# Hymba layer on one core: two partial-sum copies swap tiles every other step, gate sigmoids one slot earlier in the second half

## The chip, the cores and the metric

One Trainium2 chip, one of its cores. The metric is the device time of one execution in microseconds (us); a kernel's time is the median of its runs. The engines are TensorE (PE for its matmuls, PEld for its weight loads), VectorE (DVE), ScalarE (ACT), GpSimd (POOL) and SyncE (SP, which here issues almost all DMAs). Every engine works through its own instructions in the order in which the program lists them; an instruction that waits holds back all that stand behind it on its engine.

## What is computed

A decoder layer with two groups of token mixers (sequence 2048, width 1024, float32). The shapes: x is 2048 x 1024, w_in 1024 x 6144, w_out 2048 x 1024.

```python
xn = rms_norm(x, ln_g)
b_gate, c_gate, x_conv, g_conv, x_lru, g_lru = split(xn @ w_in)      # six of 1024 columns
y_conv = b_gate * causal_conv3(c_gate * x_conv)
u = causal_conv4(x_lru) + lru_conv_b
r = sigmoid(block_diag(u, w_a) + b_a); i = sigmoid(block_diag(u, w_i) + b_i)   # 16 heads of 64
a = exp(8 * r * log_sigmoid(lam))
h_t = a_t * h_{t-1} + sqrt(1 - a_t^2) * (i_t * u_t)                  # scan over the sequence
y = concat(head_norm(y_conv) * silu(g_conv), head_norm(h) * silu(g_lru))
out = rms_norm(x + y @ w_out, final_g)
```

## The kernel before

**Steps.** The work is a list of steps, numbered n. The first 48 are the input projection: 24 for the first half of the sequence and 24 for the second. They come in triples `l`, `a`, `b`, eight triples to a half (k = 0 to 7): `l` makes 128 channels of x_lru and g_lru, `a` of c_gate and x_conv, `b` of b_gate and g_conv. Sixteen steps of kind `o` follow, the output projection. Everything is channels by time, so a step's result is two blocks of 128 channels by 1024 positions. Its four quarters are named 11, 12 (the first block, first and second 512 positions), 21 and 22 (the second block).

**A step is a 2 x 2 block product by Winograd's form of Strassen's scheme:** seven products numbered 0 to 6 rather than eight, on sums and differences of blocks. The left blocks (weights, tiles `s`, a ring of 7) and the right blocks (activations, tiles `th` and `tl`) are each split into a high and a low part, so that a product is 4 x 3 = 12 matmuls of 128x128 by 128x512 (line 924, `mm`). One product takes one *slot* of the loop. In an ordinary step the slots s = 0 to 6 do product 0, product 6 *of the step before*, then 1, 3, 2, 4, 5. The first three of a step go into PSUM bank `A` one upon the other, and the partial sums of the scheme are copied out of it by ACT on the way:

- after product 0 into `q1` (line 1229),
- after product 1 into `u2` (line 1232; the page calls this tile `u`, and so also another tile of that name, the recurrence's),
- after product 2 into `rr` (line 1235).

DVE reads these copies when it puts the quarters together (`put`): quarter 22 is bank `B` plus `rr`, in slot 4; 11 is `C` plus `q1`, in slot 5; 21 is `B` plus `u2` when product 6 is in, which is in slot 1 *of the next step*. Each of the three copies has one tile (`sm(tag)`: a pool with one buffer per name). So the copy into `u2` in slot 2 of a step may start only when DVE has made quarter 21 of the step before, and as bank `A` is added to further, product 2 on PE (slot 4) starts only after that copy has read it. DVE's quarter 21 appears in the profile as `gl<-bank,u`, `xx<-bank,u`, `gb<-bank,u` or `ob<-bank,u` (after an `l`, `a`, `b` or `o` step).

A few steps at a change of the right blocks run otherwise: one with eight plain block products and no partial sums (`opens`), and the one behind it, with six slots (`late`).

**Order of everything else.** The scheduler is told to keep the order in which the code is written. `tick()` at the start of each slot runs what has fallen due: `at(n, f)` runs f at the n-th tick from now, and things due at one tick run in the order in which they were registered. Then come the preparations of the next step's left blocks (`prep`: in the first half ACT casts and DVE or POOL subtractions, with the split tiles stored to `sd`; in the second half mostly loads of `sd`), then the slot's matmuls, then the copy or `put`.

**The gates.** When `put(12)` of an `l` step is done (its slot 6), `lru` books its whole recurrence by such ticks (lines 753 to 759): the convolution at 1 to 3, `sth` and `stl` (the split of u into tiles `st`, ACT and DVE) at 5 and 6, `gates(0)` at 8, `sigs(0)` at 9, `gates(1)` at 10, `sigs(1)` at 11, then tanh, exp, sqrt and the scan. Tick 8 is slot 0 of the `b` step, tick 11 its slot 3. `gates(i)` is four matmuls into two PSUM tiles (line 704, pool `pss`, two buffers); `sigs(i)` is four sigmoids on ACT, r, i, r, i (line 711), the first two reading the first of these tiles and the last two the second. `gates(1)` takes the same two PSUM buffers, so it waits for `sigs(0)`.

A SiLU gate is a sigmoid on ACT (`sg`, line 637), two ticks after quarter 21, and a multiplication on POOL (`gb<-gb,sg`, `gl<-gl,sg`).

Of the kernel before, what the change touches and what calls it, by code (L numbers as in the profile page):

```python
# [38 lines left out]
def hymba_kernel(ctx: ExitStack, tc: tile.TileContext, x, xt, w_in, par, lamc, w_gate, w_out, final_g, out):  # L39
# [282 lines left out]
    def hl_done(n):  # L322
        hlc[0] -= n
# [338 lines left out]
    def lru(h, k, late=0):  # L662
        o1 = wt("o1", "xl", n=N2 + 4)
        g = wt("o2", "gl", bufs=O2)
        if h == 0:
            nc.gpsimd.memset(o1[:, 0:4], 0.0)
        else:
            nc.scalar.copy(o1[:, 0:4], hx[:, k, :])
        v = {}
        lw = [pt[:, LW + 8 * j + k:LW + 8 * j + k + 1] for j in range(4)]  # L670

        def c0():
            v["u"] = wt("u", "u")
            nc.scalar.activation(out=v["u"], in_=o1[:, 1:1 + N2], func=AF.Identity, scale=lw[0],  # L674
                                 bias=pt[:, LB + k:LB + k + 1])

        def cj(j):
            nc.vector.scalar_tensor_tensor(out=v["u"], in0=o1[:, 1 + j:1 + j + N2], scalar=lw[j],  # L678
                                           in1=v["u"], op0=ALU.mult, op1=ALU.add)

        def keep():
            if h == 0:
                nc.scalar.copy(hx[:, k, :], o1[:, N2:N2 + 4])

        def sth():
            v["st"] = st = hl_tile("st", 2)
            at(6, lambda: hl_done(2))
            for j, hi in enumerate((LO, HI)):
                nc.scalar.copy(st[j][hi], v["u"][hi])

        def stl():
            st = v["st"]
            for j, (hi, lo) in enumerate(((LO, HI), (HI, LO))):
                tt(st[j][lo], v["u"][hi], st[j][hi].bitcast(F32), ALU.subtract)

        def gates(i):
            sl = slice(i * C, (i + 1) * C)
            if i == 0:
                v["r"], v["i"] = wt("r", "r"), wt("ig", "i", bufs=IG)
            v["ps"] = ps = []  # L700
            for j in range(2):
                ps.append(pss.tile([P, C], F32, tag="s", name="gate"))
                for n in range(2):
                    nc.tensor.matmul(ps[j], v["gw"][n][:, j, :], v["st"][j][:, sl],  # L704
                                     start=(n == 0), stop=(n == 1))

        def sigs(i):
            sl = slice(i * C, (i + 1) * C)
            for j, (hi, lo) in enumerate(((LO, HI), (HI, LO))):
                for g_, src, bias in ((v["r"], hi, BA), (v["i"], lo, BI)):  # L710
                    nc.scalar.activation(out=g_[hi, sl], in_=v["ps"][j][src], func=AF.Sigmoid,  # L711
                                         bias=pt[src, bias + k:bias + k + 1])


        def s0():
            tt(v["u"], v["i"], v["u"], ALU.mult)

        def s1():
            v["T"] = wt("ig", "T", bufs=IG)
            nc.scalar.activation(out=v["T"], in_=v["r"], func=AF.Tanh, scale=nklam[:, k:k + 1])  # L720

        def s1b():
            nc.scalar.activation(out=v["r"], in_=v["r"], func=AF.Exp, scale=klam[:, k:k + 1])

        def s2():
            nc.scalar.activation(out=v["T"], in_=v["T"], func=AF.Sqrt)

        def s3():
            nc.vector.scalar_tensor_tensor(out=v["u"], in0=v["r"], scalar=1.0, in1=v["u"],
                                           op0=ALU.add, op1=ALU.mult)  # L730

        def s4():
            tt(v["u"], v["T"], v["u"], ALU.mult)

        def s5():
            r = v["r"]
            init = 0.0 if h == 0 else hl[:, k:k + 1]
            nc.vector.tensor_tensor_scan(out=r, data0=r, data1=v["u"], initial=init,
                                         op0=ALU.mult, op1=ALU.add)
            if h == 0:  # L740
                nc.vector.tensor_copy(hl[:, k:k + 1], r[:, N2 - 1:N2])

        def out_():
            finish(0, h, KT + k, v["r"], g, pt[:, LG + k:LG + k + 1])

        def gw():
            v["gw"] = load_gate_w(k)

        def put(which, bank, other):
            dst = {11: o1[:, 4:4 + C], 12: o1[:, 4 + C:4 + N2], 21: g[:, 0:C], 22: g[:, C:N2]}[which]  # L750
            combine(dst, bank, other)
            if which == 12:
                at(1, c0)
                at(2, lambda: cj(1), lambda: cj(2), keep, gw)
                at(3, lambda: cj(3))
                for slots, *fs in ((5, sth), (6, stl), (8, lambda: gates(0)), (9, lambda: sigs(0)),
                                   (10, lambda: gates(1)), (11, lambda: sigs(1)), (12, s1, s0),
                                   (13, s1b), (14, s2, s3), (15, s4), (16, s5), (17, out_)):
                    at(slots + late, *fs)
            if which == 21:  # L760
                silu(g, late)

        return put
# [71 lines left out]
    sm_u2 = [None]  # L835
# [96 lines left out]
    def sm(tag):  # L932
        return small.tile([P, C], F32, tag=tag, name=tag)
# [29 lines left out]
    with tc.manual_schedule(engines={ENG.PE, ENG.Activation, ENG.DVE, ENG.Pool, ENG.SP}):  # L963
# [182 lines left out]
        for n in range(PLAIN, N):  # L1146
            kind, h, k = steps[n]
# [27 lines left out]
            slots = (0, 6) + ORDER[1:] if not late else AFTER  # L1175
            for s in range(6 if late else 8 if new or last else 7):
                i = slots[s]
                place[0] = {"l": 0, "a": 7, "b": 14}.get(kind, 0) + s
                tick()
                if soon and s == 3:  # L1180
                    T2 = {}
                    change = Change(set_of(n + 2), T2)
                if soon and s > 3:
                    change.slot(s - 8)
                if new:
                    change.slot(s)
                if late:
                    change.slot(16 + s)
                    if s == 0:
                        prep(n, 7)  # L1190
                elif n > 0 and opens(n - 2):
                    if s == 0:
                        prep(n, 5)
                        prep(n, 6)
                    elif s == 2:
                        prep(n, 7)
                elif s == 0:
                    prep(n, 6)
                elif s == 2:
                    prep(n, 7)  # L1200
                if new and s > 0:
                    if s in (1, 3, 4, 5):
                        prep(n + 1, (1, 3, 4, 5).index(s) + 1)
                    elif s > 5:
                        prep(n + 2, s - 5)
                elif s > 0:
                    prep(n + 1, s - 1)
                if s == 3:
                    load_next(n + 2)
                if s == 1 and not late:  # L1210
                    if pend is not None:
                        S6, B, put0, u20 = pend
                        alone = B is None
                        if alone:
                            B = bank()
                        for j in range(NB):
                            mm(B, S6, T, 6, j, alone and j == 0, j == NB - 1, not alone)
                        put0(21, B, u20)
                        pend = None
                    continue  # L1220
                b = {0: "A", 1: "A", 2: "A", 5: "D" if late else "A", 3: "B", 6: "B", 4: "C"}[i]
                first = b not in bk
                if first:
                    bk[b] = bank()
                for j in range(NB):
                    mm(bk[b], S_, T, i, j, first and j == 0, j == NB - 1, not first)
                if i == 0:
                    q1 = sm("q1")
                    nc.scalar.copy(q1, bk["A"])  # L1229
                elif i == 1:  # L1230
                    u2 = sm_u2[0] = sm("u2")
                    nc.scalar.copy(u2, bk["A"])  # L1232
                elif i == 2:
                    rr = sm("rr")
                    nc.scalar.copy(rr, bk["A"])  # L1235
                    put(22, bk["B"], rr)
                    if late:
                        put(12, bk["D"], rr)
                elif i == 4:
                    put(11, bk["C"], q1)  # L1240
                elif i == 5 and not late:
                    put(12, bk["A"], None)
                elif i == 6:
                    put(21, bk["B"], u2)
# [50 lines left out]
```

## Time and profile before

| | |
|---|---|
| median of 3 runs | 1357.18 us (1356.16 to 1359.64) |
| the profiled execution, its own time | 1361.65 us |
| its span, first to last instruction | 1359.8 us |
| mean granted TensorE clock | 0.989 |
| PE busy in the span | 1301.9 us (96%) |
| DVE, ACT, POOL busy | 1032.5, 748.4, 226.2 us |
| bytes moved | 355.28 MB, 77.1% of the 16 DMA engines' time |

The durations below are from the profiled execution. It took 4.5 us longer than the median of the runs, and 1.85 us of its time lie outside the span. In rows of the trace the first number is the start in us, the second the duration; a bracket at the end gives the idle time of that engine before the row and what ended it. A row of the waits gives who waited for whom, the total in us, how many times, and the longest. A row of a table by stretch gives, behind the stretch and its length, the busy us and instruction counts of PE, PEld, DVE, ACT and POOL, the granted clock, the DMA share and GB/s.

### The profile page before, as it was taken

To read this page: it belongs to the slowest core of one execution; us is meant where nothing else is said; L and a number is where in the kernel's file an instruction comes from. 1 tells how busy PE (TensorE), PEld (TensorE's weight loads), DVE (VectorE), ACT (ScalarE), POOL (GpSimd) and SP (SyncE) were. 2 spreads that over 40 slices of the span, in tenths; PEclk is the share of its full clock that TensorE was granted. 3 is DMA by queue.
4 is the path that set the end of the run, shared out by engine and by line. 5 is a ranking of instruction groups with operands and counts; after the bars stand their busy time and mean duration, and the time that the engine had idled before them with its cause. 6 is when DMAs were issued, how large, how long until landed. Compare 5 with 4: busy or idle time off the path is not lost.

```text
span 1359.8 us, 16618 instructions
## 1 busy us (share of the span) xinstructions
PE 1301.9 (96%) x5648; PEld 1058.6 (78%) x5648; DVE 1032.5 (76%) x1245; ACT 748.4 (55%) x1139; POOL 226.2 (17%) x160
## 2 busy tenths in 40 slices
PE   6989999999999999899999999999999799998997
PEld 5867877777878787777888888888878688887886
DVE  7778788789989897978566676667458776759885
ACT  7475757575665757565544645364456233444443
POOL 3204242333334340101010110101000000000000
PEclk9989999999999999999999999999999899999999
DMA  7137797988879888542789999999778889797643
GB/s 284 31 119 258 270 252 273 278 296 302 319 281 330 291 291 304 173 162 79 247 304 286 335 354 331 332 339 365 228 253 313 249 236 227 271 404 260 240 146 136
DMA packets 158805, 355.28 MB, mean 261 GB/s; under 512 B 17920, under 2 KB 52736, under 8 KB 158720
## 3 DMA queue, kind: packets, MB, share of 16 engines
q1 hardware_dynamic: 158432, 353.90, 77.1%
q8 instruction: 45, 0.74, 0.2%
q14 instruction: 40, 0.33, 0.1%
q10 hardware_dynamic: 288, 0.32, 0.1%
HBM read 217.11 MB, written 137.04 MB: 260 GB/s over the span
## 4 chain that ended last, share of the span: by engine, by line
PE 40%; DMA 7%; DVE 4%; ACT 3%; issue 1%; SPq 0%; DVEq 0%; ACTq 0%
PE bank L924 40%; DMA traw<-td 1%; DMA zr<-rsd 1%; PE gate L704 1%; ACT i L711 1%; ACT r L711 1%; DVE tl L163 1%; DMA traw<-in_w_out_dram 1%; DMA od<-xr 1%; DMA xr<-od 1%; DVE s L163 1%; DMA xr<-in_x_dram 1%; ACT th L435 1%; DMA yd<-gl 0%; DMA raw<-yd 0%
## 5 line engine op out<-in xcount | busy, mean ns | idle before, releaser
L924 PE MATMUL bank<-th,s 128*128 128x512 f32 x3632 | 1138.8, 392 | 19.9 <-ACT u L1232 10.0
L924 PEld LDWEIGHTS bank<-th,s 128*128 128x128 f32 x3632 | 686.1, 189 | 173.5 <-ACT u L1232 15.0
L924 PE MATMUL bank<-tl,s 128*128 128x512 f32 x1816 | 711.1, 392 | 1.6 <-DVE tl L163 1.3
L924 PEld LDWEIGHTS bank<-tl,s 128*128 128x128 f32 x1816 | 343.2, 189 | 74.8 <-DVE tl L163 3.5
L163 POOL TENSOR_TENSOR s<-raw,s 128x512 fp32r<-128x512 f32 x62 | 110.2, 1790 | 253.9 <-ACT s L200 210.7
L200 ACT CAST s<-raw 128x512 fp32r<-128x512 f32 x140 | 84.5, 616 | 75.4 <-PE bank L924 41.8
L163 DVE TENSOR_TENSOR tl<-traw,th 128x512 fp32r<-128x512 f32 x117 | 85.1, 763 | 40.4 <-ACT th L435 30.0
L1232 ACT COPY u<-bank 128x512 f32<-128x512 f32 x58 | 34.0, 586 | 145.6 <-PE bank L924 77.8
L163 DVE TENSOR_TENSOR s<-s,s 128x512 fp32r<-128x512 f32 x105 | 95.5, 909 | 10.5 <-ACT s L200 10.5
L163 POOL TENSOR_TENSOR gb<-gb,sg 128x1024 f32<-128x1024 f32 x16 | 40.6, 2537 | 348.3 <-ACT sg L637 328.2
L163 DVE TENSOR_TENSOR s<-raw,s 128x512 fp32r<-128x512 f32 (+1 forms) x125 | 92.7, 765 | 6.5 <-ACT s L982 4.4
L200 ACT CAST s<-s 128x512 fp32r<-128x512 f32 x105 | 64.7, 616 | 30.3 <-DVE s L163 25.8
L435 ACT CAST th<-traw 128x512 fp32r<-128x512 f32 x96 | 55.1, 618 | 30.7 <-DMA traw<-td 17.8
L1229 ACT COPY q<-bank 128x512 f32<-128x512 f32 x58 | 33.9, 584 | 68.0 <-PE bank L924 59.2
L678 DVE SCALAR_TENSOR_TENSOR u<-xl,pt,u 128x1024 f32<-128x1024 f32 x48 | 62.7, 1306 | 6.3 <-ACT u L674 5.7
L163 DVE TENSOR_TENSOR raw<-raw,zr 128x512 f32<-128x512 f32 x64 | 41.2, 684 | 34.6 <-DMA zr<-rsd 31.1
L1235 ACT COPY rr<-bank 128x512 f32<-128x512 f32 x58 | 33.8, 583 | 50.4 <-PE bank L924 50.4
L788 DVE SCALAR_TENSOR_TENSOR t<-p,pt,t 128x1024 f32<-128x1024 f32 x32 | 46.5, 1454 | 5.9 <-ACT t L785 5.1
L163 DVE TENSOR_TENSOR st<-u,st 64x1024 fp32r<-64x1024 f32 x32 | 46.5, 1452 | 1.0
L711 ACT ACTIVATE r<-gate,pt 64x512 f32<-64x512 f32 x64 | 43.8, 684 | 3.1 <-PE gate L704 2.4
L163 POOL TENSOR_TENSOR gl<-gl,sg 128x1024 f32<-128x1024 f32 x16 | 40.4, 2523 | 24.5 <-ACT sg L637 24.5
L711 ACT ACTIVATE i<-gate,pt 64x512 f32<-64x512 f32 x64 | 43.8, 684 | 1.1
(153 smaller groups left out, 1153.7 us busy)
## 6 DMA issues: line engine op xcount, KB each, us to landing
sd<-s SPq DMA_DIRECT2D x151, 512.0 KB
s<-sd SPq DMA_DIRECT2D x151, 512.0 KB
raw<-in_w_in_dram SPq DMA_DIRECT2D x104, 256.0 KB
raw<-yd SPq DMA_DIRECT2D x64, 256.0 KB
traw<-in_w_out_dram SPq DMA_DIRECT2D x64, 256.0 KB
so<-so SPq DMA_DIRECT2D x22, 512.0 KB
s<-so SPq DMA_DIRECT2D x22, 512.0 KB
yd<-gl SPq DMA_DIRECT2D x32, 256.0 KB
```

The costliest lines, as they stand in the source:

```text
L163: (eng or nc.vector).tensor_tensor(out=out, in0=a, in1=b, op=op)
L200: nc.scalar.copy(dst[i][0], val(i))
L435: nc.scalar.copy(self.dst[i, j][0], self.r[i, j])
L678: nc.vector.scalar_tensor_tensor(out=v["u"], in0=o1[:, 1 + j:1 + j + N2], scalar=lw[j], in1=v["u"], op0=ALU.mult, op1=ALU.add)
L704: nc.tensor.matmul(ps[j], v["gw"][n][:, j, :], v["st"][j][:, sl], start=(n == 0), stop=(n == 1))
L711: nc.scalar.activation(out=g_[hi, sl], in_=v["ps"][j][src], func=AF.Sigmoid, bias=pt[src, bias + k:bias + k + 1])
L788: nc.vector.scalar_tensor_tensor(out=tcur["t"], in0=p[:, 2 + j:2 + j + N2], scalar=cw[j], in1=tcur["t"], op0=ALU.mult, op1=ALU.add)
L924: nc.tensor.matmul(bank, a[:, js], b, start=start and n == 0, stop=stop and n == 2, skip_group_check=more)
L1229: nc.scalar.copy(q1, bk["A"])
L1232: nc.scalar.copy(u2, bk["A"])
L1235: nc.scalar.copy(rr, bk["A"])
```

## The change

Two edits. In odd steps the two tiles of the third and fourth copies change places: `u2` is kept in the tile `rr`, and `rr` in the tile `u2`. And with h = 1 (the second half of the sequence) the two calls of `sigs` are booked one tick earlier, at 8 and 10, which are the ticks of `gates(0)` and `gates(1)`; as they are registered behind these, they stand behind them.

```diff
-                for slots, *fs in ((5, sth), (6, stl), (8, lambda: gates(0)), (9, lambda: sigs(0)),
-                                   (10, lambda: gates(1)), (11, lambda: sigs(1)), (12, s1, s0),
+                for slots, *fs in ((5, sth), (6, stl), (8, lambda: gates(0)), (9 - h, lambda: sigs(0)),
+                                   (10, lambda: gates(1)), (11 - h, lambda: sigs(1)), (12, s1, s0),
...
-                    u2 = sm_u2[0] = sm("u2")
+                    u2 = sm_u2[0] = sm(("u2", "rr")[n % 2])
                     nc.scalar.copy(u2, bk["A"])
                 elif i == 2:
-                    rr = sm("rr")
+                    rr = sm(("rr", "u2")[n % 2])
                     nc.scalar.copy(rr, bk["A"])
```

No instruction is added or taken away. On PE, POOL and SP the order is the same row for row. On ACT and DVE the first edit changes names only: this is ACT in step 3, the first step with seven products (`s<-raw`, `s<-s` are casts of left blocks, `xrow` is the norm of later rows, `r<-r` a square for the head norm):

```order
 L200 CAST s<-raw 128x512 x2
-L1232 COPY u_1075<-bank 128x512
+L1232 COPY rr<-bank 128x512
 L200 CAST s<-s_1051 128x512
 L534 ACTIVATE xrow,ss_615<-xrow 128x1024
 L200 CAST s<-raw 128x512
-L1235 COPY rr<-bank 128x512
+L1235 COPY u_1122<-bank 128x512
 L629 ACTIVATE r<-r 128x1024
```

The place in the order stays, the tile is the other one. This is DVE some way behind it, in slot 1 of step 4, where quarter 21 of step 3 is made:

```order
 L163 TENSOR_TENSOR s_1201<-s_1199,raw 128x512
-L163 TENSOR_TENSOR gl<-bank,u_1075 128x512
+L163 TENSOR_TENSOR gl<-bank,rr 128x512
 L678 SCALAR_TENSOR_TENSOR u<-xl,pt,u 128x1024
 L163 TENSOR_TENSOR s<-s_1051,s 128x512
```

It now reads the tile `rr`, while the next copy of `u2`, in slot 2 of step 4, writes the tile `u2`, whose last reader was earlier work; what now writes the tile `rr` after this reading is the copy of step 4 in its slot 4.

The second edit moves instructions on ACT alone. This is ACT in slots 0 to 3 of a `b` step of the second half, before (`so<-s` casts a left block of the output projection, `t<-p` is the first product of the short convolution):

```order
L395 CAST so<-s_6337 128x512
L1229 COPY q_6452<-bank 128x512
L711 ACTIVATE r<-gate,pt 64x512
L711 ACTIVATE i<-gate,pt 64x512
L711 ACTIVATE r<-gate,pt 64x512
L711 ACTIVATE i<-gate,pt 64x512
L785 ACTIVATE t<-p,pt 128x1024
L1232 COPY u_6499<-bank 128x512
L711 ACTIVATE r<-gate,pt 64x512
L711 ACTIVATE i<-gate,pt 64x512
L711 ACTIVATE r<-gate,pt 64x512
L711 ACTIVATE i<-gate,pt 64x512
```

And the same place now:

```order
L711 ACTIVATE r<-gate,pt 64x512
L711 ACTIVATE i<-gate,pt 64x512
L711 ACTIVATE r<-gate,pt 64x512
L711 ACTIVATE i<-gate,pt 64x512
L395 CAST so<-s_6337 128x512
L1229 COPY q_6456<-bank 128x512
L711 ACTIVATE r<-gate,pt 64x512
L711 ACTIVATE i<-gate,pt 64x512
L711 ACTIVATE r<-gate,pt 64x512
L711 ACTIVATE i<-gate,pt 64x512
L785 ACTIVATE t<-p,pt 128x1024
L1232 COPY rr<-bank 128x512
```

Each group of four sigmoids went ahead of the copy that used to stand before it: the first ahead of `q1` and a cast, the second ahead of `t<-p` and of the copy of `u2`.

## The prediction

> **What bounds the kernel now.** I read the page's busy line first, then a table by stretch for one triple of steps in each half, then who waits for whom, then the single stalls.
>
> ```profile
> PE 1301.9 (96%) x5648; PEld 1058.6 (78%) x5648; DVE 1032.5 (76%) x1245; ACT 748.4 (55%) x1139; POOL 226.2 (17%) x160
> 280.00:340.70 60.70, 59.85 (x262) 48.56 (x261) 56.39 (x58) 38.48 (x57) 23.23 (x16) 1.00 0.86 305
> 759.70:819.40 59.70, 59.48 (x263) 48.84 (x262) 40.72 (x47) 30.47 (x41) 6.69 (x4) 1.00 0.95 339
> ```
>
> PE bounds it everywhere, but not alone. A triple of the first half takes 60.7 us and DVE is busy for 56.4 of them; one of the second half takes 59.7, with DVE at 40.7 and ACT at 30.5. 262 matmuls in 59.85 us are 0.23 us each; a start-to-start distance above that is lost. So the change can give back only the stalls between matmuls, and in the first half DVE stands close behind.
>
> ```profile
> PE bank L924 <- ACT u L1232: 10.0, 10, 3.8
> PE gate L704 <- ACT i L711: 3.2, 14, 0.3
> PE norm_ps L582 <- DVE rt L163: 7.1, 1, 7.1
> ACT u L1232 <- DVE gb L163: 27.5, 6, 4.7
> ACT u L1232 <- DVE gl L163: 22.3, 6, 5.9
> ACT u L1232 <- DVE ob L163: 17.8, 6, 4.0
> ```
>
> The first two rows are what the two edits aim at. The last three are the same thing one engine earlier: 18 of the 58 copies of `u2` sat waiting until DVE had read the old `u2`, 67.6 us on ACT. Only part of it reaches PE.
>
> **The first edit, by its places.** It takes the three DVE rows away: the new copy writes a tile whose reader ran in slot 4 of the step before. What it adds is that the copy in slot 4 now writes what DVE reads in slot 1. The longest of these waits was 5.9 us, a part of it before product 1 had even ended; the copy in slot 4 comes two slots later, each 12 x 0.23 = 2.7 us, and DVE's reading keeps its place. I cost it at nothing; what covers it are these two slots. The largest stall of the kind, in step 4:
>
> ```profile
> 127.79 0.39 PE L924 MATMUL bank<-th,s 128*128 128x512 f32 x1
> 130.07 0.50 PE L924 MATMUL bank<-th,s 128*128 128x512 f32 x1 [1.89 <-ACT u L1232]
> 135.68 0.62 PE L924 MATMUL bank<-th,s 128*128 128x512 f32 x2
> 128.66 0.68 DVE L163 TENSOR_TENSOR gl<-bank,u 128x512 f32<-128x512 f32 x1
> 129.43 0.59 ACT L1232 COPY u<-bank 128x512 f32<-128x512 f32 x1 [5.91 <-DVE gl L163]
> 132.00:133.00 1.00, 1.00 (x4) 0.73 (x3) 1.00 (x1) 0.99 (x2) 1.00 (x2) 0.50 1.00 401
> 129.25 1.28 DVE L678 SCALAR_TENSOR_TENSOR u<-xl,pt,u 128x1024 f32<-128x1024 f32 x1
> 131.38 2.10 ACT L689 CAST st<-u 64x1024 fp32r<-64x1024 f32 x2
> 136.06 2.47 DVE L163 TENSOR_TENSOR st<-u,st 64x1024 fp32r<-64x1024 f32 x2
> 140.00 0.40 PE L704 MATMUL gate<-st,bh 128*128 128x512 f32 x1
> ```
>
> 127.79 to 130.07 is 2.28, less 0.23 is 2.05 us lost. Then the clock is granted at 0.50: from 130.07 to 135.68 stand 17 matmuls, which at 0.23 would take 3.9 of the 5.6 us, 1.7 more. Together 3.8. What is late next are the gates. Their `st` on ACT needs `u` of DVE (done at 130.5) and so can start only 0.9 sooner than 131.38; with one cast and the `rr` copy behind it, which no longer waits for PE, DVE's `st` ends some 1.6 us sooner, at 136.9. PE would be at the gates at 140.0 - 3.8 = 136.2, and their second pair at 136.7, needing the second `st`: it waits some 0.2 to 0.5. I take 3.3, between ends of 2.0 (the stall without the slow clock, should that come elsewhere) and 3.8.
>
> On that slow stretch the Trainium skill ("TensorE: Matmul & The Clock Gate", What's actually happening) says the array falls to half clock after an idle window of about 3.4 us. Here 2.05 us were enough, so the row differs; by the page this term would be 2.05 less 0.5.
>
> ```profile
> 172.04 0.39 PE L924 MATMUL bank<-th,s 128*128 128x512 f32 x1
> 173.47 0.50 PE L924 MATMUL bank<-th,s 128*128 128x512 f32 x1 [1.04 <-ACT u L1232]
> 236.10 0.50 PE L924 MATMUL bank<-th,s 128*128 128x512 f32 x1 [1.04 <-ACT u L1232]
> 251.31 0.62 ACT L200 CAST s<-s 128x512 fp32r<-128x512 f32 x1 [4.28 <-DMA sd<-s]
> ```
>
> The next two lose 1.43 - 0.23 = 1.20 each. Behind the second ACT waits for a store (last row), and PE for ACT; if the store doesn't come sooner, that wait eats the gain. Ends 0 and 2.4; I take 1.2, the middle, since stores are issued behind DVE's subtractions, which move with the rest only in part.
>
> From 280 us on four triples are alike; the first, and the stall of the fourth:
>
> ```profile
> 299.88 0.39 PE L924 MATMUL bank<-th,s 128*128 128x512 f32 x1
> 300.69 0.50 PE L924 MATMUL bank<-th,s 128*128 128x512 f32 x1 [0.42 <-ACT u L1232]
> 482.81 0.50 PE L924 MATMUL bank<-th,s 128*128 128x512 f32 x1 [0.41 <-ACT u L1232]
> 299.28 0.69 DVE L163 TENSOR_TENSOR gb<-bank,u 128x512 f32<-128x512 f32 x1
> 300.05 0.59 ACT L1232 COPY u<-bank 128x512 f32<-128x512 f32 x1 [4.56 <-DVE gb L163]
> 303.55 2.49 DVE L163 TENSOR_TENSOR s<-s,s 128x512 fp32r<-128x512 f32 x1 [0.53 <-ACT s L200]
> 303.09 2.41 POOL L163 TENSOR_TENSOR gb<-gb,sg 128x1024 f32<-128x1024 f32 x1 [5.00 <-DVE xcol L547]
> 328.94 0.47 PE L704 MATMUL gate<-st,bh 128*128 128x512 f32 x1 [0.26 <-DVE st L163]
> ```
>
> Lost are 0.81 - 0.23 = 0.58 us. If only PE came sooner, it would wait so much longer at the gates, where DVE's `st` is already the last (328.94: 0.26 idle, and 0.17 more as every idle time is 0.17 less than the loss, 0.58 against 0.42). But DVE, busy all the way from the `rr` copy of the `b` step to that `st`, has one idle time in it, the 0.53 before 303.55, and that is a wait for ACT, which was held up by the copy at 300.05. With ACT up to 2.5 us ahead it goes too. So PE and DVE both come 0.55 sooner: 4 x 0.55 = 2.2. Ends: 0 (DVE gains nothing), and 4 x (0.58 + 0.43) = 4.0 (DVE gains so much that the gates don't wait either).
>
> In the output steps the `ob` waits (17.8 us on ACT) stand against no PE row of `u` but one, the 3.8 us. There the copy was held by a cast that stood ahead of it, waiting for DVE, not by the tile:
>
> ```profile
> 1229.12 0.62 ACT L200 CAST s<-s 128x512 fp32r<-128x512 f32 x1 [3.32 <-DVE s L163]
> ```
>
> I cost both at nothing; what covers the `ob` waits is the slot between copy and product 2.
>
> **The second edit.** The second half's triples all show this in slots 0 to 2 of the `b` step:
>
> ```profile
> 823.94 0.59 ACT L1229 COPY q<-bank 128x512 f32<-128x512 f32 x1 [3.15 <-PE bank L924]
> 824.54 0.69 ACT L711 ACTIVATE r<-gate,pt 64x512 f32<-64x512 f32 x1
> 826.66 0.68 ACT L711 ACTIVATE i<-gate,pt 64x512 f32<-64x512 f32 x1
> 826.66 0.40 PE L704 MATMUL gate<-st,bl 128*128 128x512 f32 x1
> 827.40 0.50 PE L704 MATMUL gate<-st,bh 128*128 128x512 f32 x1 [0.34 <-ACT i L711]
> 648.46 0.50 PE L704 MATMUL gate<-st,bh 128*128 128x512 f32 x1 [0.22 <-ACT i L711]
> 1006.42 0.50 PE L704 MATMUL gate<-st,bh 128*128 128x512 f32 x1 [0.34 <-ACT i L711]
> 1018.90 0.50 PE L924 MATMUL bank<-th,s 128*128 128x512 f32 x1 [0.68 <-ACT rr L1235]
> ```
>
> ACT sits idle for 3.15 us waiting for product 0, copies `q1`, and only then runs the four sigmoids, although the gates were on PE a slot earlier. The last ends at 827.34, after PE has reached the second pair of `gates(1)`: 827.40 - 826.66 - 0.23 = 0.51 us lost. Moved ahead of `q1`, the four (2.8 us) fill the 3.15: they start some 0.7 after the first gate, end about 3.5 after it, and `q1` is ready at 4 x 0.23 + 2.7 + 0.2 = 3.9, so it isn't delayed by more than a cast that may stand between (0.6); PE needs it only a slot later. There are seven such stalls, three of 0.22 idle (the first at 648.46) and four of 0.34 (the last at 1006.42): 3 x 0.39 + 4 x 0.51 = 3.2 us. Lower end 7 x 0.39 = 2.7.
>
> The second group goes ahead of `t<-p` and of the copy of `u2`. It starts 0.7 into slot 2, ends at 3.5, `t<-p` (1.15) at 4.6, the copy at 5.2; product 2 needs it at 4 x 0.23 + 2 x 2.7 = 6.4. So 1.2 us of slack are left where there were 1.9, and in the one triple with eight more casts on ACT, the last, about as much. There the row at 1018.90 lost 0.68 + 0.17 = 0.85 because ACT was behind with casts it had put off; with the sigmoids sooner in ACT's idle time it isn't. I take 0.8; ends 0 and 0.85. No DMA, no SP and no POOL instruction is moved by this edit, and the DVE product `u<-i,u` stays at tick 12.
>
> **The sum.** 3.3 + 1.2 + 2.2 + 3.2 + 0.8 = 10.7 us. Against the profiled execution 1361.65 - 10.7 = 1350.9; that one stands 4.5 us above the median, and I carry the gain over unchanged: 1357.2 - 10.7 = 1346.5. With all upper ends 3.8 + 2.4 + 4.0 + 3.2 + 0.85 = 14.2, so 1342.9; with all lower ends 2.0 + 0 + 0 + 2.7 + 0 = 4.7, so 1352.5.
>
> **The rivals.**
>
> *DVE holds the first half.* Its 56.4 of 60.7 us and the `st` row at 328.94 speak for it, the 0.53 idle against it. Then the terms 1.2 and 2.2 turn into longer waits at the gates, and the sum is 2.0 to 3.3 + 3.2 + 0.8: about 1350.5.
>
> *The gain ends at a transfer.* Where the right blocks change, PE waits for DVE and DVE for loads (the 7.1 us before `norm_ps`). Were these loads fixed in time, what was gained ahead of them would be lost there: 1357, no change. Against it: SP issues them in program order behind the work that moves, and the DMA share, 0.95 in the row at 759.70, is high but not full.
>
> *Slower: POOL lands on DVE.* At 303.55 a DVE subtraction took 2.49 us where its like at 299.28 took 0.69, exactly while POOL ran `gb<-gb,sg` (303.09 to 305.50). With ACT ahead, `sg` and so this product start up to 2 us sooner, and the casts that set off POOL's subtractions too. Each further product that catches DVE costs up to 2.41 us, and in the first half DVE's lateness reaches PE in full. One more in each of seven triples is 16.9, less the 0.53 idle each (3.7), against the 3.3 + 3.2 + 0.8 that stay: 1357.2 - 7.3 + 13.2 = 1363. It decides from 1.6 us more of blocking a triple on. Against it: the same product hits DVE now, so moving it mostly moves the hit. The Trainium skill ("SBUF — State Buffer", Who interferes with whom) has this as an exclusive lock between VectorE and GpSimd that whoever starts first holds for the whole instruction, and the 2.49 agrees.
>
> **Chances.** The sum as worked out, 1341 to 1350: 0.65. DVE holds the first half, 1350 to 1353: 0.20. Ends at a transfer, 1353 to 1361: 0.10. Slower, over 1361: 0.05. A measurement of this kernel tells some 0.3% from no change, 4.1 us (the runs of before lie 3.5 apart). So faster by more takes the first case and nearly all of the second, 0.83; within it 0.12; slower 0.05. The range 1341 to 1353 takes the first two cases and a little of what a run varies by.
>
> **What would show it.** In the trace after: no row in which ACT's `u` or `rr` copy at line 1232 waits for DVE `gb`, `gl` or `ob`; PE's wait for line 1232 down from 10.0 us to little more than the 3.8 of the output steps; PE's wait for ACT `i` only in the first half, seven of 14; triples of the second half at 59.2 us and of the first at 60.1; no half clock near 131 us. It would be wrong if the waits of `gate` for DVE `st` grow by what the copies gave back, if a wait of PE for `q1` appears in the `b` steps of the second half, or if the DVE rows beside POOL's get longer.

## The result, and the profile after

The changed kernel takes 1349.0 us (1348.61 to 1350.76), the kernel before took 1358.41 (1356.16 to 1359.81): a ratio of 0.9934, 95% interval 0.9917 to 0.995, and 9.4 us between the medians. A second timing gave 1350.09 against 1360.01, 0.9926 (0.9913 to 0.9939). Predicted were 1346.5 and a gain of 10.7. The profiled execution after took 1349.16 us. Its page's busy line:

```profile
PE 1297.1 (96%) x5648; PEld 1058.9 (79%) x5648; DVE 1034.7 (77%) x1245; ACT 748.3 (56%) x1139; POOL 231.1 (17%) x160
```

The instructions are the same in number, and POOL is busier by 4.9 us for the same work; this is the first sign of what ate part of the gain. In the experiments below it holds for every trace with the swap that keeps the products on POOL (229.1 to 231.1 us, 226.2 to 227.5 without the swap). DVE's 2.2 us more are no sign: a second trace of the kernel before has it busy for 1037.1. The table by stretch, for the same triples as before and the slow spot of step 4:

```profile
275.50:335.85 60.35, 59.88 (x262) 48.62 (x261) 56.63 (x58) 38.71 (x57) 23.71 (x16) 1.00 0.86 307
754.10:813.25 59.15, 59.15 (x262) 48.86 (x261) 38.78 (x45) 30.46 (x42) 6.59 (x4) 1.00 0.93 338
131.00:132.00 1.00, 1.00 (x6) 0.84 (x5) 1.00 (x3) 0.99 (x2) 0.92 (x2) 1.00 0.06 25
```

A triple of the second half went from 59.7 to 59.15 us, and PE has no idle time left in it. One of the first half went from 60.7 only to 60.35. The clock is at 1.00 at 131 us. Who waits for whom, on PE:

```profile
PE norm_ps L582 <- DVE rt L163: 6.1, 1, 6.1
...
PE bank L924 <- ACT rr L1232: 4.4, 2, 3.9
PE gate L704 <- DVE st L163: 4.3, 8, 1.1
...
PE bank L924 <- ACT rr L1235: 1.4, 3, 0.7
PE gate L704 <- ACT i L711: 1.2, 7, 0.2
...
PE bank L924 <- ACT u L1235: 0.7, 1, 0.7
```

The wait for line 1232 fell from 10.0 to 4.4 us, nearly all of it the one of the output steps, and the wait for the sigmoid `i` from 14 times to seven. But the gates now wait 4.3 us for `st`, where the two traces of the kernel before have 2.9 and 2.0, and the waits for the copy of line 1235 grew from 1.0 to 2.1. (The copies of `u2`, line 1232, and of `rr`, line 1235, are the third and the fourth copy, as in the section on the change. Their tiles change places in odd steps: `rr L1235` and `u L1235` are the same copy.)

Where the time went is read best from landmarks on PE: the start of the gates near 87, 146 and 274 us, of the last ones of each half, of the first matmul of `norm_ps`, which stands just ahead of the wait there, and of the last matmul. (These gates are each time the second group, `gates(1)`.) A stage is the time from one landmark to the next; what PE loses within the gates of a landmark belongs to the stage behind it. The first landmark is taken behind a stretch in which the clock is granted at 0.50; every trace has it, and it ends at 80 to 85 us, differently in each execution. With four traces without the swap and five with it, and three without the sooner sigmoids and six with them (all kernels here that keep the products on POOL), the means in us are, with the gains taken before rounding:

| stage | term | without the edit | with it | gain | predicted |
|---|---|---|---|---|---|
| 87 to the gates at 146 | step 4 | 59.3 (59.6, 59.6, 59.6, 58.3) | 58.0 (58.0 each) | 1.3 | 3.3 |
| to the gates at 274 | two triples | 125.5 (127.8, 124.8, 124.8, 124.7) | 124.5 (123.9 to 124.8) | 1.0 | 1.2 |
| to the last gates of the first half | four alike triples | 242.7 (242.6 to 242.8) | 241.3 (241.2 to 241.3) | 1.4 | 2.2 |
| second half to its last gates | six of the gate stalls | 487.9 (487.6 to 488.4) | 484.9 (484.4 to 485.6) | 3.0 | 2.7 |
| last gates to `norm_ps` | seventh gate stall, last triple | 52.0 (51.7 to 52.5) | 50.3 (49.9 to 51.3) | 1.7 | 1.3 |
| wait at `norm_ps`, output steps | | 296.0 (294.8 to 297.1) | 295.8 (293.1 to 297.3) | 0.3 | 0 |

They add up to 8.7 us. The swap gives 3.7 of it where 6.7 were predicted, the sigmoids 4.8 where 4.0 were (the last two terms of the sum, 3.2 and 0.8, spread over two stages). The rest of the measured 9.4 to 9.9 lies within what single executions differ by.

### The profile page after: what moved, and what is told of

The parts are those of the page before. It is cut to its first block, busy times and chain, and to the rows that moved or that the text cites. A ratio compares the mean times of both kernels' runs of the same rounds, so it can differ in the third digit from the quotient of the medians.

```text
span 1347.4 us, 16571 instructions
## 1 busy us (share of the span) xinstructions
PE 1297.1 (96%) x5648; PEld 1058.9 (79%) x5648; DVE 1034.7 (77%) x1245; ACT 748.3 (56%) x1139; POOL 231.1 (17%) x160
## 4 chain that ended last, share of the span: by engine, by line
PE 45%; DMA 6%; DVE 3%; ACT 1%; issue 1%; SPq 0%; DVEq 0%; ACTq 0%
PE bank L924 44%; DMA traw<-td 3%; DMA zr<-rsd 1%; PE gate L704 1%; DMA od<-xr 1%; DVE tl L163 1%; DVE s L163 0%; DVE raw L163 0%; DMA yd<-gl 0%; DMA s<-so 0%; DVE ob L163 0%; DMA yd<-gb 0%; ACT th L435 0%; DVE st L163 0%; DVE gl L619 0%
## 5 line engine op out<-in xcount | busy, mean ns | idle before, releaser
L163 POOL TENSOR_TENSOR gb<-gb,sg 128x1024 f32<-128x1024 f32 x16 | 43.4, 2712 | 332.4 <-ACT sg L637 293.8
L163 DVE TENSOR_TENSOR s<-raw,s 128x512 fp32r<-128x512 f32 (+1 forms) x125 | 89.9, 742 | 8.3 <-ACT s L982 4.4
L163 DVE TENSOR_TENSOR s<-s,s 128x512 fp32r<-128x512 f32 x105 | 84.5, 805 | 4.1 <-ACT s L200 4.1
L1229 ACT COPY q<-bank 128x512 f32<-128x512 f32 x58 | 33.9, 584 | 50.3 <-PE bank L924 43.7
L163 DVE TENSOR_TENSOR st<-u,st 64x1024 fp32r<-64x1024 f32 x32 | 50.0, 1562 | 1.0
L1232 ACT COPY rr<-bank 128x512 f32<-128x512 f32 x31 | 18.1, 584 | 51.8 <-PE bank L924 51.8
L163 DVE TENSOR_TENSOR raw<-raw 128x512 f32<-128x512 f32 x41 | 44.5, 1085 | 0.2
```

What stands on the lines that cost most here:

```text
L163: (eng or nc.vector).tensor_tensor(out=out, in0=a, in1=b, op=op)
```

## The experiments

**Each edit alone.** My theory by then: the swap's gain was cut down because DVE and POOL now meet more often in the first half.

```diff
 swap alone
-                    u2 = sm_u2[0] = sm("u2")
+                    u2 = sm_u2[0] = sm(("u2", "rr")[n % 2])
-                    rr = sm("rr")
+                    rr = sm(("rr", "u2")[n % 2])
 sigmoids alone
-        ... (9, lambda: sigs(0)), (10, lambda: gates(1)), (11, lambda: sigs(1)), ...
+        ... (9 - h, lambda: sigs(0)), (10, lambda: gates(1)), (11 - h, lambda: sigs(1)), ...
```

The swap:

> Only the first edit: the tiles of the third and fourth copies change places in odd steps; the sigmoids stay where they were. Theory (the two edits act on different halves and add up): all of the lead at 640 us stays, about 7 us by the two traces, or about 5 if the stall for a store near 250 us (2.6 us and 1.4 of slow clock) is no part of it, so 0.9948 to 0.9963 of before; the seven waits of the gates for the sigmoid i in the second half come back (0.22 to 0.34 idle each). Rival (the lead of the first half is lost where the right blocks change, and what was measured comes from the sigmoids): 0.998 or more. Rival (the edits need each other): the remainder differs from the sum by over 2 us.

Measured: 1357.33 us against 1360.77, ratio 0.9978 (0.9965 to 0.999): 3.0 us by the ratio. That is short of the 5 to 7 us of the theory and just under the first rival's 0.998, but not for the rival's reason: the second half takes 487.9 us here and 487.6 in a trace of the kernel before, so no lead is lost where the right blocks change. What is missing is missing in the first half already. In its waits the long list for line 1232 is gone but for three, and the 14 waits for `i` are all there:

```profile
PE bank L924 <- ACT rr L1232: 6.3, 3, 4.3
...
PE gate L704 <- DVE st L163: 4.6, 8, 1.5
PE gate L704 <- ACT i L711: 3.2, 14, 0.3
```

The sigmoids:

> Only the second edit: sigmoids of the gates a slot sooner in the second half; the copies keep their tiles. Theory: the seven stalls go (0.39 or 0.51 each, 3.2 us), 0.1 more a triple (0.6), and 0.8 to 1.5 in the last triple: 4 to 5 us, 0.9964 to 0.997 of before. Rival (ACT's copies come later and PE waits for them instead): under 2 us, 0.9985 or more.

Measured: 1353.41 us, ratio 0.9945 (0.9931 to 0.996), 7.4 us. That is more than the 4 to 5 expected, and more than its profiled execution shows (4.5 us less than that of the second trace of the kernel before, below), so both it and the whole change were timed again, beside each other:

> The second edit alone once more, beside the unedited changed kernel on the same chip, to settle what each edit is worth. By the traces (time from the last gates of the first half to norm_ps: 487.9 and 52.0 us without the edit, 485.0 and 50.2 with it) the second edit is worth 4.5 to 4.7 us: about 1355.5 us, ratio 0.9965. By the medians of the first timing it is worth 7.4 us: 1352.5 to 1353.5, ratio 0.9945.

> The changed kernel, unedited, beside the second edit alone. By the traces the swap takes the first half from 436.5 to some 433 us, so this kernel should stand 3 to 4 us under the second edit alone: 1349 to 1350.5 if that gives 1353, 1351.5 if it gives 1355.5. By the first timings only 1.6 us lie between the two (0.9945 and 0.9934).

Measured: 1354.41 us, 0.9956 (0.9941 to 0.997), and 1350.09 us, 0.9926 (0.9913 to 0.9939). So the sigmoids alone are worth 5.6 us here, between the two figures expected, and the swap on top of them 4.3. The two estimates of the sigmoids' worth, 7.4 and 5.6, have intervals that overlap; the traces' 4.8 lies in the second only.

**The kernel before, a second trace.** Its first trace has a stall of 2.63 us at 249.6, behind a store, and a slow clock after it; is that the kernel or the run?

> The kernel before, once more, for a second trace. If the wait for a store near 250 us and the slow clock behind it belong to the order of the work, they are here again at the same place to within a few us, with 2.5 us idle; if they are chance, they are gone or elsewhere, and the gain between the two profiled executions (12.5 us) holds up to 4.3 us that the change did not make.

Measured: 1359.82 us. The stall is 1.25 us here, without the slow clock, and the stage to 274 takes 124.8 rather than 127.8. So 3 us of the difference between the first two traces belong to that one execution, and without it the table's second line is 124.75 against 124.5: 0.2 us gained.

**Why the swap gave half.** In step 4 the stall of 2.05 us is gone. These are PE, DVE and POOL of the kernel after behind it:

```profile
133.22 0.39 PE L924 MATMUL bank<-th,s 128*128 128x512 f32 x1
134.12 0.50 PE L924 MATMUL bank<-th,s 128*128 128x512 f32 x1 [0.51 <-ACT rr L1235]
...
137.25 0.40 PE L704 MATMUL gate<-st,bl 128*128 128x512 f32 x1
138.79 0.47 PE L704 MATMUL gate<-st,bh 128*128 128x512 f32 x1 [1.14 <-DVE st L163]
134.82 3.82 DVE L163 TENSOR_TENSOR st<-u,st 64x1024 fp32r<-64x1024 f32 x2
132.49 2.84 POOL L163 TENSOR_TENSOR gl<-gl,sg 128x1024 f32<-128x1024 f32 x1
135.28 2.28 POOL L163 TENSOR_TENSOR s<-raw,s 128x512 fp32r<-128x512 f32 x1
```

Two new stalls: 0.90 - 0.23 = 0.67 and 1.54 - 0.23 = 1.31, together 1.98 of the 2.05 us that were saved. `st` on DVE takes 3.82 us where it took 2.47, beside two POOL instructions. What is left of this term is nearly all the slow clock, and that comes only in some executions. In the second run of the sigmoids alone, which has the stall as before, PE, the table by stretch, DVE and POOL show:

```profile
127.35 0.39 PE L924 MATMUL bank<-th,s 128*128 128x512 f32 x1
129.62 0.50 PE L924 MATMUL bank<-th,s 128*128 128x512 f32 x1 [1.88 <-ACT u L1232]
131.00:132.00 1.00, 1.00 (x6) 0.82 (x5) 1.00 (x2) 0.99 (x3) 0.97 (x1) 1.00 0.48 193
134.92 3.60 DVE L163 TENSOR_TENSOR st<-u,st 64x1024 fp32r<-64x1024 f32 x2
136.15 1.29 POOL L163 TENSOR_TENSOR s<-raw,s 128x512 fp32r<-128x512 f32 x1 [1.25 <-ACT s L200]
```

The clock stayed at 1.00, PE loses only 0.27 us more up to the end of the gates at 138.7, and the stage took 58.3 us, 0.3 more than with the swap. `st` took 3.60 here, without the swap: it starts sooner than at 136.06 as the clock is up, and so meets POOL's subtraction. The lengthening goes with the sooner start, then, and not with the swap as such. In the other three traces without the swap the clock fell, as in the first run of the sigmoids alone, and the stage took 59.6:

```profile
132.00:133.00 1.00, 1.00 (x4) 0.79 (x3) 1.00 (x2) 0.99 (x2) 1.00 (x2) 0.50 0.87 348
```

In the alike triples POOL's product `gb<-gb,sg` moved. After, then in the second trace of the kernel before:

```profile
295.55 2.88 POOL L163 TENSOR_TENSOR gb<-gb,sg 128x1024 f32<-128x1024 f32 x1 [3.05 <-ACT sg L637]
296.09 2.88 DVE L163 TENSOR_TENSOR raw<-raw 128x512 f32<-128x512 f32 x1
299.05 0.62 ACT L200 CAST s<-raw 128x512 fp32r<-128x512 f32 x1 [2.12 <-issue]
299.58 0.57 ACT L1235 COPY rr<-bank 128x512 f32<-128x512 f32 x1
```

```profile
298.53 0.69 DVE L163 TENSOR_TENSOR raw<-raw 128x512 f32<-128x512 f32 x1
300.40 2.49 DVE L163 TENSOR_TENSOR s<-s,s 128x512 fp32r<-128x512 f32 x1 [0.53 <-ACT s L200]
299.94 2.41 POOL L163 TENSOR_TENSOR gb<-gb,sg 128x1024 f32<-128x1024 f32 x1 [5.00 <-DVE xcol L547]
```

With ACT ahead, the sigmoid and so the product start sooner. Before, it caught the subtraction `s<-s`, which took 2.49; now it catches `raw<-raw` two rows ahead, 2.88 instead of 0.69. That is so in each of the four triples of all five traces with the swap, and in none of the four without it. ACT's next cast reads that `raw`, and the fourth copy (`rr`) stands behind this cast, so PE waits for it: 0.23 us lost a triple, in place of the 0.56 to 0.58 for the third copy. (The idle of 2.12 is put down to "issue", but the cast starts 0.08 us after `raw` ends at 298.97.)

**Taking POOL's product away.** If that is the cause, the same kernel with both SiLU products on DVE must give the swap's gain back, though DVE gets more to do:

```diff
-        at(4 + late, lambda: tt(g, g, sg[0], ALU.mult, nc.gpsimd))
+        at(4 + late, lambda: tt(g, g, sg[0], ALU.mult))
```

> The changed kernel, with the SiLU products (gb<-gb,sg and gl<-gl,sg) on DVE instead of POOL. Theory (what the first edit gave up, it gave up because POOL's product, now sooner, holds a DVE operation: 2.88 us instead of 0.69 at 296 us, st 3.82 instead of 2.47 at 135 us): DVE pays 1.2 us for each product but is no longer held for 1.8 to 2.2, so the waits of the gates for st shrink from 4.3 us to under 2.5 and the copy rr no longer stalls PE (0.7 at 176 and 238 us): 2 to 5 us faster than the changed kernel, 0.990 to 0.992 of before. Rival (DVE is simply full in the first half): DVE's 2.4 us more a triple come out at the gates, 5 to 12 us slower than the changed kernel, 0.997 to 1.003 of before.

Measured: 1340.48 us (1340.11 to 1341.69), ratio 0.9853 (0.9837 to 0.9869). That is 8.5 us under the changed kernel, where the theory expected 2 to 5 and the rival a loss. The waits of the gates for `st` shrank from 4.3 to 0.8 us, as the theory said. By stages the trace gains 1.3, 2.3 and 3.4 us in the first half and 1.2 in the second, against the means above. Then the same without the swap:

> The changed kernel with both SiLU products on DVE instead of POOL, but without the swap of the two tiles. With the swap and the products on DVE the ratio was 0.9853 (1340.48 us); the swap alone was worth 0.9978, about 3 us. Theory (the swap is worth only 3 us because ACT, set free earlier, starts POOL's product onto DVE's work): with POOL's product gone the swap should be worth nearly all the u stalls, about 2.0 + 1.2 + 1.2 + 4 x 0.55 = 6.6 us, so this kernel takes about 1347 us, ratio 0.989 to 0.991, and the stalls of the third copy (line 1232) stand in its trace. Rival (POOL has nothing to do with it; the first half is held by DVE's own work): the swap is worth about 3 us here too or less, 1343.5 us or under, ratio 0.9875 or below.

Measured: 1344.44 us, ratio 0.989 (0.9876 to 0.9903). Without POOL's product the swap is worth 4.0 us by the medians and 5.0 by the ratios (the two kernels ran beside different runs of the kernel before), where 6.6 had been expected by the theory and 3 or less by the rival. By the traces the four alike triples go from 241.6 to 237.9 us, where on POOL they go from 242.7 to 241.3. The table by stretch for one such triple, without the swap and with it:

```profile
326.65:386.85 60.20, 59.62 (x261) 48.65 (x261) 54.57 (x59) 38.48 (x57) 18.99 (x13) 1.00 0.88 308
```

```profile
326.00:385.47 59.47, 59.30 (x261) 48.72 (x260) 54.49 (x59) 38.71 (x57) 18.59 (x13) 1.00 0.88 311
293.74 0.69 DVE L163 TENSOR_TENSOR raw<-raw 128x512 f32<-128x512 f32 x1
297.31 1.22 DVE L163 TENSOR_TENSOR gb<-gb,sg 128x1024 f32<-128x1024 f32 x1
```

0.73 us a triple rather than 0.35: the collision did eat half of it there. DVE does two products more a triple and yet is busy 54.5 us rather than 56.6, since `raw<-raw` is back at 0.69 and the product takes 1.22 on DVE, where it blocked DVE for some 2.2 from POOL; other rows that POOL's products held are shorter, too. So DVE's own work does not hold the alike triples, and for them the rival falls. In the stage of step 4 the swap brings 0.75 us here (56.70 against 57.45): with it PE still waits there 0.77 us for `st`, which takes 3.45 us. POOL's subtraction stands beside it, for 2.01 us, as it did after; that wasn't tried apart. The two triples give 1.9 us (122.2 against 124.1). So by the traces the swap is worth 6.4 us in the first half, close to the theory's 6.6; in the second half the kernel with it takes 0.9 us longer (483.7 against 482.8), with a slow clock behind the stall at the change of the right blocks that the other trace doesn't have. This fits a whole between the theory's figure and the rival's, but it is one trace of each.

**Which group of sigmoids, and the spread of the wait at `norm_ps`.** Only `sigs(0)` sooner, and the changed kernel once more, one execution each:

```diff
-        ... (10, lambda: gates(1)), (11 - h, lambda: sigs(1)), ...
+        ... (10, lambda: gates(1)), (11, lambda: sigs(1)), ...
```

> The changed kernel with only the first group of four sigmoids (sigs(0)) sooner in the second half, the second at its old place. Theory: the seven gate stalls come from the first group alone and stay gone; the stall of the last triple for the rr copy near 1010 us (0.85 us lost in the kernel before) was the second group's doing and is back; about 1350 us in one run. Rival: that stall went with the first group too, or is not tied to either; then this run shows no stall there and about 1349 us.

> The changed kernel once more, unedited, for the spread from run to run. The wait of norm_ps for DVE rt was 8.52 and 7.1 us in two runs of the kernel before and 6.13 us in one of the kernel after. If the 1 to 2.4 us belong to the change, it is again about 6.1 here (5.5 to 6.7); if it varies by itself, anything from 5 to 8.5. Time 1348 to 1351 us.

Measured: 1352.41 and 1350.07 us, single executions (the first has the longest last stage of all, 297.3 us, which varies by 4 us among the traces with the sooner sigmoids). With the first group alone the seven gate stalls are gone, and the stall of the last triple, which I had tied to the second, is gone too: the rival holds. Its stages behind the first half are those of the whole change (484.6 and 50.2 us), so the second group is worth nothing that the trace shows. The wait at `norm_ps` was 5.1 us in the second trace of the changed kernel and 7.0 with the first group alone, against 6.1 in the first trace; before, 7.1 and 8.5. So this wait moves by 2 us by itself and shows nothing. The stage ahead of it does (51.7 to 52.5 against 49.9 to 51.3).

The 1.7 us of that stage are stalls of PE. In the second trace of the kernel before, then at the same gates with the sigmoids alone:

```profile
1001.57 0.40 PE L704 MATMUL gate<-st,bl 128*128 128x512 f32 x1
1002.31 0.50 PE L704 MATMUL gate<-st,bh 128*128 128x512 f32 x1 [0.34 <-ACT i L711]
1002.65 0.39 PE L704 MATMUL gate<-st,bl 128*128 128x512 f32 x1
...
1014.79 0.50 PE L924 MATMUL bank<-th,s 128*128 128x512 f32 x1 [0.69 <-ACT rr L1235]
1015.13 0.39 PE L924 MATMUL bank<-tl,s 128*128 128x512 f32 x1
...
1014.17 0.57 ACT L1235 COPY rr<-bank 128x512 f32<-128x512 f32 x1
```

```profile
999.47 0.40 PE L704 MATMUL gate<-st,bl 128*128 128x512 f32 x1
999.70 0.39 PE L704 MATMUL gate<-st,bh 128*128 128x512 f32 x1
999.93 0.39 PE L704 MATMUL gate<-st,bl 128*128 128x512 f32 x1
...
1008.61 0.59 ACT L1235 COPY rr<-bank 128x512 f32<-128x512 f32 x1
```

The first is the seventh gate stall, 0.74 - 0.23 = 0.51 us, the second that of the fourth copy in the last triple, 0.84 (the matmul ahead of it starts at 1013.72). And behind each stall the next start is late as well: 0.34 us where 0.23 is usual. That is 0.1 us a stall, or 0.6 and 0.95 us for these two, and with the sooner sigmoids both are gone. PE's lead of the one trace on the other, 2.1 us at the last gates, is 3.8 at the first matmul of `norm_ps`; ACT's, at the fourth copy, is 5.6.

**The best version.** Both products on DVE, and the sigmoids a slot sooner in the first half as well:

```diff
-        ... (9 - h, lambda: sigs(0)), (10, lambda: gates(1)), (11 - h, lambda: sigs(1)), ...
+        ... (8, lambda: sigs(0)), (10, lambda: gates(1)), (10, lambda: sigs(1)), ...
-        at(4 + late, lambda: tt(g, g, sg[0], ALU.mult, nc.gpsimd))
+        at(4 + late, lambda: tt(g, g, sg[0], ALU.mult))
```

> The changed kernel with both SiLU products on DVE, and the sigmoids of the gates one slot sooner in the first half as well. What is left there are seven stalls of PE for the sigmoid i, 0.33 us lost each with the products on DVE: 2.3 us. Theory A (ACT has the idle time in the first half too): they go, 1338.2 us, ratio 0.983 to 0.984. Theory B (in the first half ACT's casts stand between and DVE and the rr copy come later for it): 1340 us or more, ratio 0.985 or above, with PE waiting for a copy of the left blocks or for rr instead.

Measured: 1336.44 us (1335.83 to 1338.13), ratio 0.9835 (0.9821 to 0.9848), the fastest of all, though its interval overlaps that with the products on DVE alone (0.9837 to 0.9869), so that the last 2 us are not certain. The waits for `i` are gone from the trace and an alike triple takes 59.10 us where nothing comes between (59.47 with the products on DVE alone); one of four takes 61.10, with a wait for `q1` and one for `st` in it. So theory A holds in the plain triples, B in one of them, and all four together take 238.8 us against 237.9. What this trace gains lies elsewhere: 2.9 us in the two triples, 1.75 of them from a shorter stall for `q1` near 245 us, and 3.5 in the second half, which the edit doesn't touch, with a stall of 1.7 rather than 3.3 us at the change of the right blocks. Whether these belong to the edit or to the execution stays open.

## Why the prediction was right or wrong

The sign and the two mechanisms were right, but 10.7 us of gain against 9.4 to 9.9 looks closer than it was, and the closeness is luck: the swap gave 3.0 alone and 4.3 on top of the sigmoids, where 6.7 were predicted, and the sigmoids gave more than their 4.0. The first is one error, made three times: durations on DVE were carried over from the trace before.

- **Step 4 (3.3 predicted, 1.3 found).** The step that failed is "DVE's `st` ends some 1.6 us sooner, at 136.9". It ended at 138.64: it started at 134.82, but beside POOL it took 3.82 us. I had taken its duration from before, 2.47, and moved only its start. The stall of 2.05 turned into 0.67 + 1.31, and the slow clock, which I took as certain, came in three of four executions. Where it didn't come, the swap gains 0.3 us, and not the 2.0 that I had as the lower end for this.
- **Two triples (1.2 and 1.0).** The size is near by chance: it holds the one store stall of the first trace, and without that 0.2 are left. What eats the gain isn't the store that I named, but waits for the fourth copy (0.88 and 0.87 lost in place of 1.20 and 1.20) and for `st` (2.4 to 2.8 lost in place of 0.9 to 1.3). With the products on DVE these waits are gone.
- **Four alike triples (2.2 and 1.4).** "DVE has one idle time in it, with ACT ahead it goes too" came true, but left out that the same lead starts POOL's product sooner, onto another DVE row. This row is held for 2.19 us where the other was held for 1.80, DVE is busy for 56.6 us a triple rather than 56.4, and so 0.35 of the 0.55 are left. I had it as the rival "POOL lands on DVE", and set it aside with "moving it mostly moves the hit". It does move the hit, to a place with PE close behind: right in kind, wrong in that a moved hit costs nothing.
- **The seven gate stalls (3.2 predicted, 3.6 found: 3.0 for six and 0.6 for the last), no delay of `q1`.** Right. The sum counted only one late start a stall; the next one is 0.1 us late, too. The sigmoids now stand in ACT's idle time, and `q1` waits for the last of them for 0.32 us that PE doesn't see:

```profile
814.26 0.68 ACT L711 ACTIVATE i<-gate,pt 64x512 f32<-64x512 f32 x1
815.26 0.59 ACT L1229 COPY q<-bank 128x512 f32<-128x512 f32 x1 [0.32 <-ACT i L711]
```

- **The last triple (0.8 and 0.95).** The stall went as said, though with the first group of sigmoids. The rest of what this stage gained is the seventh gate stall.
- **Rivals.** "DVE holds the first half", about 1350.5, comes nearest in time, and half of its reason is right: in the alike triples DVE has no idle time left after, so what it does sets the pace. But it isn't full of its own work, it is held by POOL: with the products given to it, it is busy for less and the first half got faster. "The gain ends at a transfer" doesn't show: PE's lead is not lost at the change of the right blocks, nor up to `norm_ps`.

Of the signs named for the trace, the missing waits of the copies, line 1232, the seven waits for `i`, 59.2 us in the second half and the clock at 131 came as said; 60.1 in the first half did not, and two of the signs of being wrong showed in part: the waits for `st` grew, though by 1.4 to 2.3 us and not by all that the copies gave back, and of the DVE rows beside POOL's `st` in step 4 and `raw<-raw` got longer, while one `s<-s` row a triple got shorter.

The Trainium skill ("SBUF — State Buffer", Who interferes with whom) says that a VectorE instruction with two SBUF inputs and a GpSimd one that reads SBUF exclude each other for a whole instruction, by the order of issue. The row of `raw<-raw`, 2.88 beside POOL's 2.88 and 0.69 without it, agrees. By that rule, any term that moves DVE or POOL has to be costed with the new overlaps, which the sum did not do.

## What to carry to other kernels

When a stall is taken away, list not only what then comes sooner on the engine that waited, but what that engine sets off, and look for each of these on which instruction of a neighbour it will now fall; a duration measured beside other work is not a property of the instruction. Where one engine's work holds up another's, as POOL's did DVE's here, a product moved off the busy engine can cost it more (some 2.2 us) than doing it itself (1.22). And take two traces of the kernel before, before costing a stall or a slow clock that one trace shows.

## What the hardware showed

Moving work to the busiest helper made that helper less busy: DVE's 32 more instructions came with a busy time of 1027.0 us instead of 1033.7 to 1034.7 in the three traces of the changed kernel.

The slow clock is not set by the length of a stall alone. After 2.05 us it came in three of four executions. After a stall of 3.1 us at the change of the right blocks, it came in all four traces that have both the swap and sooner sigmoids with the products on POOL, and in none of the five that lack one of the two edits. With the products on DVE and the sooner sigmoids it came after 3.27 us with the swap, and not after 3.25 without it. In the kernel after, and in the second trace of the kernel before:

```profile
559.06 0.39 PE L924 MATMUL bank<-th,s 128*128 128x512 f32 x1
562.37 0.50 PE L924 MATMUL bank<-th,s 128*128 128x512 f32 x1 [2.92 <-ACT q L1229]
564.00:565.00 1.00, 1.00 (x4) 0.79 (x3) 1.00 (x2) 0.84 (x1) 0.08 (x1) 0.50 1.01 397
```

```profile
566.19 0.50 PE L924 MATMUL bank<-th,s 128*128 128x512 f32 x1 [2.94 <-ACT q L1229]
567.00:568.00 1.00, 1.00 (x6) 0.83 (x5) 1.00 (x2) 1.00 (x3) 0.14 (x1) 1.00 1.01 397
```

The Trainium skill ("TensorE: Matmul & The Clock Gate", What's actually happening) has the array fall to half clock after an idle window of about 3.4 us, in windows that run freely of the program. That it varies from run to run agrees with these rows. That a stall of 2.05 us, less than a window, is enough differs from it, and the measurement decides. What else decides between two stalls alike stays open. It costs little at 563: in four of the five traces where the clock stayed up, PE waits 1.5 to 1.6 us for the third copy some 7 us later instead.
